# Other homes for the adaLN tiles of a two-layer hybrid decoder trunk on one NeuronCore

## The chip, the cores and the metric

The kernel runs on one NeuronCore of a Trainium2 chip. The metric is device time in microseconds of one launch; the kernel before has a median of 2782.91 us over three runs (2778.63 to 2790.88). Beside these stands one profiled execution, from which all rows below come.

Names of engines: PE is TensorE's matmul, PEld its weight load, DVE is VectorE, ACT is ScalarE, POOL is GpSimd, SP is SyncE, which issues nearly all DMAs.

## The reference

Two layers, 256 tokens of width 2048, float32. Each layer is a token mixer and then a SwiGLU feed-forward, and each of these four sub-layers has an adaLN modulation:

```python
def _ada(c, w, b):
    mod = jax.nn.silu(c) @ w + b                 # w: 2048 x 6144, one for each of the 4 sub-layers
    shift, scale, gate = jnp.split(mod, 3, axis=-1)

for layer in range(2):
    shift, scale, gate = _ada(c, ada_w[layer, 0], ada_b[layer, 0])
    h = x * (1.0 + scale) + shift
    y = _mixer_ab(h, ...) if layer % 2 == 0 else _mixer_cd(h, ...)
    x = _layer_norm(ALPHA * x + (1.0 + gate) * y, ln_g[layer, 0], ln_b[layer, 0])
    shift, scale, gate = _ada(c, ada_w[layer, 1], ada_b[layer, 1])
    y = (jax.nn.silu(h2 @ wg) * (h2 @ wu)) @ wd  # h2 = x * (1 + scale) + shift; D_FF 5632
    x = _layer_norm(ALPHA * x + (1.0 + gate) * y, ln_g[layer, 1], ln_b[layer, 1])
```

The first mixer holds mLSTM heads and RWKV-7 heads, the second retention heads and gated DeltaNet heads. `c` is one row, so an adaLN product is a vector times a matrix: 6144 dot products of length 2048 for each sub-layer, and 50 MB of weights that are read for it.

## The kernel before

**Weights.** Every large product is cut into units. A unit is one weight tile of 128 x 2048 float32 (1 MiB), brought by one DMA of SP (L681, in `raw`) into a ring of three 8 KB tiles with the tag `raw`. `split` (L703, L704) cuts it into two halves; for each half ACT writes a rounded `hi` and DVE the rest `lo`, into rings of three tiles each. PE multiplies `hi` and `lo` with the split activations in three passes (`part`, L718 to L720), 24 matmuls of 512 columns for a unit. A `raw` tile is free again when the second `lo` of its unit has been made.

**adaLN.** An adaLN unit is also a tile of 128 x 2048 (128 of the 6144 dot products). `ada_unit` loads it through the same `raw` ring, and one DVE instruction (L640, SCALAR_TENSOR_TENSOR) multiplies it with `silu(c)` and sums along the row. There are 192 units, 48 to a sub-layer. They aren't done where they are used but in small portions beside the products: after each unit of a product `fill(rate)` adds `rate` to a credit, and each whole credit emits one adaLN unit. After each norm the first 8 fills are passed over. The first feed-forward has 88 units of gate and up weights (`gu`) and 44 of down weights (`dn`), in thirds of 32 + 16, 32 + 16 and 24 + 12; in the kernel before only the `gu` products fill, at a rate of 64/84. In the second mixer (68 units) the rate is 32/44 up to a limit, in the second feed-forward 16/40 up to the last of the 192.

**Small tiles.** In the mixers, `z` is a ring of six 1 KB tiles (shifted RWKV channels), `sp` one 2 KB tile (rows on their way to DRAM), and `zt` a ring of two 4 KB tiles: rows of a product before they are transposed, or a pair of `hi` and `lo` in the first units of a stage. In the feed-forwards these tiles hold nothing after the first units.

**What sets the order.** The program is written stage by stage, and then `Plan` walks over all its instructions with a table of durations and emits an order for each engine: among the ready instructions of an engine the one with the lowest priority number goes first, a tile is opened only when its ring has a free one, and a load counts as ready only with a free tile. Splits of weights have their priorities moved forward. That order is then imposed on all engines and on SP's queue, which issues its DMAs strictly in this order, each when the tile it writes is free. So an edit of tiles or rates in one place can move instructions of every engine there.

Of the kernel before, what the change touches and what calls it, by code (L numbers as in the profile page):

```python
# [207 lines left out]
class Plan:  # L208
# [3 lines left out]
    def __init__(self, tc, nc, soon=0.5):  # L212
# [3 lines left out]
        self.depend()  # L216

# [308 lines left out]
class Trunk:  # L526
# [67 lines left out]
    def setup(self):  # L594
# [25 lines left out]
        self.ada_next = self.ada_pause = 0  # L620

# [8 lines left out]
    def ada_unit(self, u, deep):  # L630
        nc, v = self.nc, self.nc.vector
        sub, i = divmod(u, 48)
        src = self.ins["ada"][u]
        if deep and i % 2:
            w = self.a8([P, D])
            nc.sync.dma_start(w[:], src)
        else:
            w = self.raw(src)
# [40 lines left out]
    def raw(self, src, room=None):  # L679
        w = room([P, 2048]) if room else self.raw_p.tile([P, 2048], F32, tag="raw", name=self.name("raw"))  # L680
        self.nc.sync.dma_start(w[:, :src.shape[-1]], src)  # L681
        return w

    def split(self, src, n, ahead=2000, homes="ss", room=None):
# [3 lines left out]
        with self.tc.high_priority(offset=ahead):  # L688
            w = self.raw(src, room)
            parts = []  # L690
            for i, home in enumerate(homes):
# [8 lines left out]
                else:  # L700
                    hi, lo = (self.own([P, 1024], "zt", 2, F32R) for _ in range(2))
# [239 lines left out]
    def ffn(self, l, x, h):  # L941
# [3 lines left out]
        rate = 64.0 / 84 if l == 0 else 16.0 / 40  # L945
# [3 lines left out]
        for third, m in enumerate(THIRDS):  # L949
# [21 lines left out]
            for n in range(4):  # L971
                u0 = l * 44 + d0 + n * m
                banks = self.product([dn[u0 + i] for i in range(m)], 512, a, 0.0, tail=FFN_TAIL if third == 2 and n == 3 else ())
# [142 lines left out]
    def by_tokens(self, banks, zt=None):  # L1116
        if zt is None:
            zt = self.own([P, NT, 512], "zt", 2)
        for t in range(NT):
            self.nc.scalar.activation(zt[:, t, :], banks[t][:], AF.Copy)  # L1120
        return zt

    def put_by(self, banks):

        dst = self.dram.tile([T, 512], F32, name=self.name("by"))
        for t in range(NT):
            s = self.own([P, 512], "sp", 1)
            self.nc.scalar.activation(s[:], banks[t][:], AF.Copy)
            self.nc.scalar.dma_start(dst[P * t:P * t + P, :], s[:])
# [8 lines left out]
    def rwkv_tiles(self, zt, block):  # L1138

        nc = self.nc  # L1140
        for i in range(0, 4, 2):
# [5 lines left out]
            for j in range(2):  # L1147
                c, what = divmod(4 * block + i + j, 3)
                m = self.rkv[c, what] = self.own([P, T], "z", 6)
                cases.append((m[:], b[:, T * j:T * j + T], (("mu_r", "mu_k", "mu_v")[what], c)))  # L1150
# [20 lines left out]
    def rwkv_front(self, B, c):  # L1171
# [20 lines left out]
        nc.scalar.activation(sq[:], km[:], AF.Square, scale=self.col("k_k", c))  # L1192
# [5 lines left out]
        v.scalar_tensor_tensor(ar[:, ct, :, 0, :], tok(km[:]), self.nkk[:, c:c + 1], gg[:, :, 0:P], ALU.mult, ALU.mult)  # L1198
        v.tensor_tensor(ar[:, ct, :, 1, :], tok(rm[:]), gg[:, :, 1:P + 1], ALU.mult)
        kp = self.f1([P, T])  # L1200
        v.tensor_scalar(kp[:], a[:], self.col("k_a", c), self.nkk[:, 8 + c:9 + c], ALU.mult, ALU.add)
        v.tensor_tensor(kp[:], kp[:], km[:], ALU.mult)
        v.tensor_tensor(bk[:, ct, 1], tok(kp[:]), gi[:], ALU.mult)
        v.scalar_tensor_tensor(a[:], km[:], self.col("k_k", c), a[:], ALU.mult, ALU.mult)
        v.tensor_tensor(bk[:, ct, 0], tok(a[:]), gi[:], ALU.mult)
        v.scalar_tensor_tensor(kp[:], rm[:], self.col("r_k", c), kp[:], ALU.mult, ALU.mult)
        b = self.bank("c")
        nc.tensor.matmul(b[:, 0:T], self.con("bones"), kp[:], start=True, stop=True)
        v.tensor_tensor(B["vb"][:, 1, ct, :], b[:, 0:T], vm[:], ALU.mult)
# [158 lines left out]
    def rwkv(self, product, early, beside, after):  # L1368

        self.rkv = {}  # L1370
# [536 lines left out]
```

## Time and profile before

| what | value |
|---|---|
| median of 3 runs | 2782.91 us |
| the profiled execution | 2782.83 us, its span 2780.7 us |
| PE busy | 2639.4 us, 95% of the span |
| DVE busy | 2010.2 us, 72% |
| ACT busy | 1265.2 us, 45% |
| first feed-forward, first to last group of its transposes (L963) | 773.9 to 1406.2 us of the span |
| second feed-forward, the same | 2078.9 to 2698.1 us |
| second mixer, products and heads | about 1490 to 1905 us |

The span is the time from the first to the last instruction; 2.1 us of the execution lie around it. Matmuls overlap, so a busy PE can still lose time between matmuls. A row of waits names the waiting instruction, the one that released it, the total in us, how often, and the longest.

### The profile page before, as it was taken

The numbers are of one execution on the slowest core, as the hardware profiler recorded it, in microseconds if no ns is written. First come the engines' busy times: TensorE is split into PE (matmuls) and PEld (weight loads), VectorE is DVE, ScalarE is ACT, GpSimd is POOL, SyncE is SP. The second block draws the span as 40 slices with busy tenths as digits, with TensorE's granted clock in tenths as the row PEclk, the third lists the DMA queues.
The fourth block names the chain that finished last, engine by engine and source line by source line (L and its number), as shares of the span: only waits on it lengthen the run. The fifth ranks groups of instructions, "written<-read, shape, count | busy, mean of one in ns | idle before, by whom it ended". The sixth has DMA issues, their size and how long they took to land.

```text
span 2780.7 us, 33791 instructions
## 1 busy us (share of the span) xinstructions
PE 2639.4 (95%) x12906; PEld 2157.6 (78%) x12906; DVE 2010.2 (72%) x3153; ACT 1265.2 (45%) x1704; POOL 78.8 (3%) x88
## 2 busy tenths in 40 slices
PE   5598999999999999999999999999999999999997
PEld 3576777788777887788888888878778888888886
DVE  7899877658777567768767898875866646557557
ACT  2364445556634444443446554444454444443442
POOL 0000000110000000000000201100000000000000
PEclk9899999999999999999999999999999999999999
DMA  9988775235578678878866776675657657666554
GB/s 394 364 295 299 261 255 208 91 107 197 199 286 318 226 266 319 317 259 309 324 232 214 257 258 228 250 268 181 232 196 270 244 197 264 220 215 237 199 183 165
DMA packets 109820, 681.61 MB, mean 245 GB/s; under 512 B 12437, under 2 KB 15705, under 8 KB 31577
## 3 DMA queue, kind: packets, MB, share of 16 engines
q1 hardware_dynamic: 108506, 677.36, 67.0%
q8 instruction: 101, 1.65, 0.2%
q10 hardware_dynamic: 1152, 2.10, 0.2%
q14 instruction: 61, 0.50, 0.1%
HBM read 668.89 MB, written 10.52 MB: 244 GB/s over the span
## 4 chain that ended last, share of the span: by engine, by line
PE 63%; DMA 10%; DVE 9%; issue 4%; ACT 3%; POOL 0%; DVEq 0%; ACTq 0%; SPq 0%; POOLq 0%
PE g L720 19%; PE g L719 19%; PE g L718 19%; DMA raw<-ada 3%; DVE lo L704 3%; DMA raw<-gu 3%; DVE raw L640 3%; DMA raw<-w_cd 2%; ACT hi L703 2%; DMA t<-x 1%; PE m L963 1%; DMA t<-lnrow 1%; DMA raw<-w_ab 1%; PE m L1231 0%; PE m L899 0%
## 5 line engine op out<-in xcount | busy, mean ns | idle before, releaser
L704 DVE TENSOR_TENSOR lo<-raw,hi 128x1024 fp32r<-128x1024 f32 (+2 forms) x802 | 971.4, 1217 | 598.5 <-ACT hi L703 594.1
L703 ACT ACTIVATE hi<-raw 128x1024 fp32r<-128x1024 f32 (+2 forms) x802 | 838.1, 1052 | 1143.6 <-PE g L720 855.6
L718 PE MATMUL g<-hi,h 128*128 128x512 f32 (+2 forms) x2312 | 908.4, 394 | 54.8 <-ACT h L782 38.4
L719 PE MATMUL g<-lo,h 128*128 128x512 f32 (+2 forms) x2312 | 909.9, 394 | 10.2 <-DVE lo L704 9.9
L720 PE MATMUL g<-hi,h 128*128 128x512 f32 (+2 forms) x2312 | 906.2, 392 | 0.0
L718 PEld LDWEIGHTS g<-hi,h 128*128 128x128 f32 x2312 | 439.7, 190 | 152.0 <-ACT h L782 41.3
L719 PEld LDWEIGHTS g<-lo,h 128*128 128x128 f32 x2312 | 440.4, 190 | 107.8 <-DVE lo L704 20.6
L720 PEld LDWEIGHTS g<-hi,h 128*128 128x128 f32 x2312 | 440.1, 190 | 86.3 <-issue 1.7
L640 DVE SCALAR_TENSOR_TENSOR raw<-raw,silu_c 128x2048 f32<-128x2048 f32 x176 | 402.6, 2287 | 31.5 <-DMA raw<-ada 22.7
L718 PE MATMUL g<-hi,a 128*128 128x512 f32 x920 | 361.0, 392 | 5.4 <-DVE t L860 5.4
L719 PE MATMUL g<-lo,a 128*128 128x512 f32 x920 | 360.0, 391 | 0.1
L720 PE MATMUL g<-hi,a 128*128 128x512 f32 x920 | 360.0, 391 | 0.0
L718 PEld LDWEIGHTS g<-hi,a 128*128 128x128 f32 x920 | 173.4, 188 | 41.7 <-DVE t L860 5.8
L719 PEld LDWEIGHTS g<-lo,a 128*128 128x128 f32 x920 | 173.5, 189 | 36.4 <-DVE lo L704 0.9
L720 PEld LDWEIGHTS g<-hi,a 128*128 128x128 f32 x920 | 173.4, 189 | 35.7
L1413 DVE SCALAR_TENSOR_TENSOR f<-c,cols_sb,f 128x253 f32<-128x253 f32 (+2 forms) x120 | 56.0, 476 | 4.7 <-ACT f L1410 3.9
L1614 POOL TENSOR_SCALAR s<-cons_sb,log_alpha 128x128 f32<-128x128 f32 x16 | 15.2, 962 | 1017.7 <-DVE log_alpha L1558 882.9
L1084 POOL TENSOR_SCALAR_AFFINE_SELECT a<-a 128x512 f32<-128x512 f32 (+1 forms) x20 | 27.3, 1372 | 323.1 <-ACT a L1233 178.7
L640 DVE SCALAR_TENSOR_TENSOR a<-a,silu_c 128x2048 f32<-128x2048 f32 x16 | 36.3, 2285 | 0.0
L902 ACT ACTIVATE t<-m,affine 128x128 f32<-128x128 f32 x96 | 35.0, 473 | 0.1
L1231 PE MATMUL m<-y 64*128 64x256 f32 x128 | 29.2, 405 | 3.8 <-DVE a L1234 3.7
L966 ACT ACTIVATE a<-m 128x512 fp32r<-128x512 f32 x44 | 26.1, 592 | 13.5 <-PE m L963 12.3
(476 smaller groups left out, 2052.9 us busy)
## 6 DMA issues: line engine op xcount, KB each, us to landing
raw<-ada SPq DMA_DIRECT2D x176, 1024.0 KB, 5.1
raw<-gu SPq DMA_DIRECT2D x176, 1024.0 KB, 4.9
raw<-dn SPq DMA_DIRECT2D x88, 1024.0 KB, 4.8
raw<-w_cd SPq DMA_DIRECT2D x60, 1024.0 KB, 4.8
raw<-w_ab SPq DMA_DIRECT2D x48, 1024.0 KB, 5.1
a<-ada SPq DMA_DIRECT2D x16, 1024.0 KB, 17.0
raw<-o_ab SPq DMA_DIRECT2D x16, 1024.0 KB, 4.8
raw<-o_cd SPq DMA_DIRECT2D x16, 1024.0 KB, 5.4
```

The lines of the kernel that those rows point to most:

```text
L640: v.scalar_tensor_tensor(w[:], w[:], 1.0, self.sc[:], ALU.mult, ALU.mult, accum_out=m[:, i:i + 1])
L703: nc.scalar.activation(hi[:, :2 * n], ws, AF.Copy)
L704: nc.vector.tensor_tensor(lo[:, :2 * n], ws, hi[:, :2 * n], ALU.subtract)
L718: mm(o, ah, wh, start=start and k == 0, stop=False)
L719: mm(o, ah, wl, start=False, stop=False)
L720: mm(o, al, wh, start=False, stop=stop and k == 3)
L902: nc.scalar.activation(h32[:, j, :], b[:, P * j:P * j + P], AF.Identity, bias=self.ab[:, sub + 1, 16 + k:17 + k], scale=self.ab[:, sub + 1 ...
L963: nc.tensor.transpose(b[:, P * k:P * k + P], gs[:, t, P * k:P * k + P], self.ident)
L966: nc.scalar.activation(act[:, 0, :, ts], bv, AF.Copy)
L1084: self.nc.gpsimd.affine_select(x, x, pattern=[[0, n] for n in dims] + [[1, P]], compare_op=ALU.is_gt if strict else ALU.is_ge, fill=0.0, b ...
L1231: mm(b[:, T * x:T * x + T], bk[r, c, x, t, :], ar[r, c, t].rearrange("p x s -> p (x s)"), start=True, stop=True)
L1413: v.scalar_tensor_tensor(o[:, d:T], b[:, T * j:T * j + T - d], self.col(wname, 4 * (tile0 + i + j) + 3 - d), o[:, d:T], ALU.mult, ALU.add)
```

## The change

Four edits, all in where tiles live and when the adaLN units are emitted:

1. The six `z` tiles and the `sp` tile become slots of one 8 KB tile `za`, and the two `zt` tiles become halves of one 8 KB tile `zt`. The order in which slots are used stays.
2. In both feed-forwards an adaLN unit is loaded into `za` or `zt` in turn and no longer into `raw`; in the second mixer every other one goes to `za`, the rest to `raw`. The first mixer keeps `raw`.
3. Such a load is tied, for the planner alone, to the weight load that stands before it in the program: it counts as ready only when that one has landed in the plan.
4. In the first feed-forward the rate falls from 64/84 to 64/100, and the `dn` products of the first third fill too (in both feed-forwards).

```diff
-    def __init__(self, tc, nc, soon=0.5):
+    def __init__(self, tc, nc, soon=0.5, after={}):
...
+        at = {x.name: i for i, x in enumerate(self.ins)}
+        for x, y in after.items():
+            self.deps[at[x]].add(at[y])
...
+        elif home == "raw":
+            w = self.raw(src)
         else:
-            w = self.raw(src)
+            w = self.own([P, D], home, 1)
+            self.after[nc.sync.dma_start(w[:], src).ins.name] = self.load
...
     def raw(self, src, room=None):
-        self.nc.sync.dma_start(w[:, :src.shape[-1]], src)
+        self.load = self.nc.sync.dma_start(w[:, :src.shape[-1]], src).ins.name
...
-                    hi, lo = (self.own([P, 1024], "zt", 2, F32R) for _ in range(2))
+                    both = self.own([P, 2, 1024], "zt", 1, F32R)
+                    hi, lo = both[:, 0], both[:, 1]
...
     def ffn(self, l, x, h):
-        rate = 64.0 / 84 if l == 0 else 16.0 / 40
+        self.homes, self.pair = ("za", "zt"), None
+        rate = 64.0 / 100 if l == 0 else 16.0 / 40
...
-                banks = self.product([dn[u0 + i] for i in range(m)], 512, a, 0.0, tail=FFN_TAIL if third == 2 and n == 3 else ())
+                banks = self.product([dn[u0 + i] for i in range(m)], 512, a, 0.0 if third else rate, tail=FFN_TAIL if third == 2 and n == 3 else ())
...
-            zt = self.own([P, NT, 512], "zt", 2)
+            zt = self.half([P, NT, 512])
...
+    def half(self, shape):
+        if self.pair is None:
+            self.pair = self.own([P, 2, 1024], "zt", 1)
+            self.turn = 0
+        self.turn += 1
+        x = self.pair[:, self.turn % 2]
...
-            s = self.own([P, 512], "sp", 1)
+            s = self.chan[:, 6:8].rearrange("p a b -> p (a b)")
...
-                m = self.rkv[c, what] = self.own([P, T], "z", 6)
+                m = self.rkv[c, what] = self.chan[:, self.made % 6]
+                self.made += 1
...
     def rwkv(self, product, early, beside, after):
+        self.chan = self.own([P, 8, T], "za", 1)
+        self.made = 0
...
     def mixer_cd(self, h, rate):
+        self.homes, self.pair = ("za", "raw"), None
```

The order moves at three places. In the rows, `raw_N<-gu` is the load of a gate or up unit, `raw_N<-ada`, `za_N<-ada` and `zt_N<-ada` are loads of adaLN units, and `lo_N<-raw_M,hi_K` is DVE's half of a split.

**First place: the first third of the first feed-forward, shortly after its first transposes.** SP's queue before:

```order
L681 DMA raw_6269<-gu 128x2048
L681 DMA raw_6303<-ada 128x2048
L681 DMA raw_6306<-gu 128x2048
L681 DMA raw_6340<-ada 128x2048
L681 DMA raw_6343<-gu 128x2048
```

The same stretch of SP's queue now (the numbers of tiles differ, since fewer are made):

```order
L690 DMA raw_6261<-gu 128x2048
L690 DMA raw_6295<-gu 128x2048
L647 DMA zt_6329<-ada 128x2048
L690 DMA raw_6337<-gu 128x2048
L690 DMA raw_6374<-gu 128x2048
L647 DMA za_6371<-ada 128x2048
```

Before, the tile of `raw_6340` is the one that `raw_6269` leaves, three loads earlier, and two of the three are adaLN's. Now the tile of `raw_6374` is the one that `raw_6261` leaves, and the three are all weights. DVE's order there before, from the last reader of `raw_6269` on (L967 is the split of the activation):

```order
L704 TENSOR_TENSOR lo_6276<-raw_6269,hi_6275 128x1024
L967 TENSOR_TENSOR a_6216<-m_6226,a_6216 128x4x128
L704 TENSOR_TENSOR lo_6309<-raw_6306,hi_6308 128x1024
L640 SCALAR_TENSOR_TENSOR raw_6340,modulation<-raw_6340,silu_c 128x2048
L704 TENSOR_TENSOR lo_6313<-raw_6306,hi_6312 128x1024
L704 TENSOR_TENSOR lo_6346<-raw_6343,hi_6345 128x1024
```

And DVE's order now, from the last reader of `raw_6261` on:

```order
L714 TENSOR_TENSOR lo_6268<-raw_6261,hi_6267 128x1024
L649 SCALAR_TENSOR_TENSOR zt_6329,modulation<-zt_6329,silu_c 128x2048
L714 TENSOR_TENSOR lo_6298<-raw_6295,hi_6297 128x1024
L714 TENSOR_TENSOR lo_6302<-raw_6295,hi_6301 128x1024
L714 TENSOR_TENSOR lo_6340<-raw_6337,hi_6339 128x1024
L649 SCALAR_TENSOR_TENSOR za_6371,modulation<-za_6371,silu_c 128x2048
L714 TENSOR_TENSOR lo_6344<-raw_6337,hi_6343 128x1024
L714 TENSOR_TENSOR lo_6377<-raw_6374,hi_6376 128x1024
```

What moved: between the row that frees a `raw` tile and the row that reads the next load of that tile stand two rows before (`raw_6340`) and six now (`raw_6374`).

**Second place: the down products of the same third.** SP's queue there held nothing but loads of `dn` before. Now:

```order
L690 DMA raw_7232<-dn 128x2048
L690 DMA raw_7270<-dn 128x2048
L690 DMA raw_7307<-dn 128x2048
L647 DMA zt_7304<-ada 128x2048
L647 DMA za_7341<-ada 128x2048
L690 DMA raw_7344<-dn 128x2048
L690 DMA raw_7378<-dn 128x2048
L690 DMA raw_7419<-dn 128x2048
L647 DMA zt_7412<-ada 128x2048
```

Ten adaLN loads stand among the 16 of `dn`, often two in a row. Over the first feed-forward it is 61 now (15, 10, 21 and 15 in the stretches `gu`, `dn`, `gu`, `gu`) and was 60 (18, none, 24, 18).

**Third place: the second mixer.** SP's queue before, in the gated DeltaNet part:

```order
L681 DMA raw_12531<-w_cd 128x2048
L681 DMA raw_12565<-ada 128x2048
L681 DMA raw_12568<-w_cd 128x2048
L681 DMA raw_12602<-ada 128x2048
L681 DMA raw_12605<-w_cd 128x2048
L681 DMA raw_12639<-w_cd 128x2048
```

And now:

```order
L690 DMA raw_12486<-w_cd 128x2048
L690 DMA raw_12520<-ada 128x2048
L690 DMA raw_12523<-w_cd 128x2048
L690 DMA raw_12560<-w_cd 128x2048
L647 DMA za_12557<-ada 128x2048
L690 DMA raw_12594<-w_cd 128x2048
```

Of 36 adaLN loads in this stage, all in `raw`, there are now 35, 18 in `raw` and 17 in `za`. The orders of PE, DVE and ACT in this stage differ in many places, and ACT loads its function tables twice more.

32 lines of the change are left out of this document (19 added, 13 removed).

## The prediction

> **What bounds the kernel now.** The first page comes first, for the engine that is busiest:
>
> ```profile
> span 2780.7 us, 33791 instructions
> PE 2639.4 (95%) x12906; PEld 2157.6 (78%) x12906; DVE 2010.2 (72%) x3153; ACT 1265.2 (45%) x1704; POOL 78.8 (3%) x88
> PE 63%; DMA 10%; DVE 9%; issue 4%; ACT 3%; POOL 0%; DVEq 0%; ACTq 0%; SPq 0%; POOLq 0%
> PE g L720 19%; PE g L719 19%; PE g L718 19%; DMA raw<-ada 3%; DVE lo L704 3%; DMA raw<-gu 3%; DVE raw L640 3%; DMA raw<-w_cd 2%; ACT hi L703 2%; DMA t<-x 1%; PE m L963 1%; DMA t<-lnrow 1%; DMA raw<-w_ab 1%; PE m L1231 0%; PE m L899 0%
> ```
>
> The chain of waits gives 3% each to adaLN loads, `gu` loads and the adaLN passes on DVE (L640), some 9% or 250 us. That isn't what removing them would bring: while the chain follows them back, PE works on units that are already in its buffers. What PE loses has to be read from PE. The kernel holds its own yardstick: the two feed-forwards do the same products, one with 60 adaLN units beside them, the other with 16. The line of their transposes (L963) marks the same place in both, here first for the first and then for the second feed-forward (count, shortest, median and longest in ns, first and last start in us), and then both stretches in busy time (PE, PEld, DVE, ACT, POOL; clock; DMA share and GB/s):
>
> ```profile
> L963 PE MATMUL m<-cons_sb,q x88: 270/272/329, 774.2 to 1407.5; 128*128 128x128 f32 x88
> L963 PE MATMUL m<-cons_sb,q x88: 270/272/332, 2079.2 to 2699.4; 128*128 128x128 f32 x88
> 773.90:1406.20 632.30, 624.82 (x2771) 511.00 (x2770) 454.40 (x446) 261.09 (x273) 0.00 (x0) 1.00 0.80 294
> 2078.90:2698.10 619.20, 619.20 (x2770) 512.33 (x2770) 356.98 (x338) 263.94 (x273) 0.00 (x0) 1.00 0.63 226
> ```
>
> The two stretches run from first to last group of the transposes, with 2,770 matmuls each and the full clock. In the second PE is busy for all of 619.2 us. The first takes 632.3 us: **13.1 us more**, of which 7.5 us show as idle PE and the rest is hidden under the overlap of matmuls. That is all that a better supply can bring there. Why it is late is told by SP's queue and by ACT, for the first stretch and then for the second:
>
> ```profile
> SPq L681 <- DVE lo L704: 348.8, 109, 6.6
> SPq L681 <- DVE raw L640: 172.1, 55, 5.7
> L703 ACT ACTIVATE hi<-raw 128x1024 fp32r<-128x1024 f32 x225 | 235.2, 1059 | 351.0 <-PE g L720 177.7 <-DMA raw<-gu 151.1 <-DMA raw<-dn 12.2
> ...
> SPq L681 <- DVE lo L704: 510.8, 111, 6.0
> SPq L681 <- DVE raw L640: 40.6, 16, 6.8
> L703 ACT ACTIVATE hi<-raw 128x1024 fp32r<-128x1024 f32 x225 | 238.8, 1061 | 352.1 <-PE g L720 350.4 <-DVE lo L704 1.7
> ```
>
> In the second feed-forward ACT waits for PE alone: the weights are there, and PE sets the pace. In the first it waits 151.1 us for `gu` loads, and SP issues loads late since 55 times the tile that is next in the ring is held by an adaLN pass. So this stage is bound by PE with a ring of three tiles that is too short for 1.7 loads per unit, by a little.
>
> **The first feed-forward.** Durations, from the same stretch:
>
> ```profile
> L704 DVE TENSOR_TENSOR lo<-raw,hi 128x1024 fp32r<-128x1024 f32 x224 | 271.3, 1223 | 160.5 <-ACT hi L703 159.1
> L640 DVE SCALAR_TENSOR_TENSOR raw<-raw,silu_c 128x2048 f32<-128x2048 f32 x60 | 137.2, 2287 | 10.0 <-DMA raw<-ada 9.3
> L967 DVE TENSOR_TENSOR a<-m,a 128x512 fp32r<-128x512 f32 x20 | 13.4, 683 | 0.0
> DMA to landing us min/median/max: 4.7/5.2/7.9
> DMA to landing us min/median/max: 4.7/6.1/8.7
> DMA to landing us min/median/max: 4.6/4.8/5.9
> ```
>
> The landings are those of adaLN loads and of `gu` loads in the first feed-forward, and of `gu` loads in the second. A unit is 2 `lo`, so each stretch holds 112 units, and PE's pace is 619.2 / 112 = 5.53 us a unit. Now the rows of the order at the first place. Before, `raw_6340` can be issued when `lo_6276` is done, and its reader stands two rows on: 0.68 + 1.22 = 1.9 us of DVE work to cover a landing of 5.2 us. `raw_6343` follows it at once and is read four rows on (a, lo, the pass, lo: 5.4 us), less 1.06 us for ACT's `hi`, against 6.1 us. Both are short, and only what PE has in its three `hi` and `lo` tiles bridges it. After the change the weight load `raw_6374` is issued when `lo_6268` is done and read six rows on: two passes and four `lo`, 2 x 2.29 + 4 x 1.22 = 9.5 us, less 1.06 for `hi`, against 6.1 us. The adaLN load behind it, `za_6371`, has four rows, 2.29 + 3 x 1.22 = 6.0 us against 5.2. Weights have 2.3 us to spare, adaLN about 0.8 us. I therefore expect this stage to run near the pace of the second feed-forward. Not all of it:
>
> ```profile
> PE g L719 <- DVE lo L704: 3.6, 8, 0.8
> PE m L963 <- DVE q L960: 2.6, 4, 1.1
> PE g L718 <- ACT hi L703: 0.7, 2, 0.4
> ```
>
> Of 6.9 us named, 2.6 us are transposes that wait for DVE's product `q`, which may stand behind an adaLN pass of 2.29 us; that stays possible at 0.64 passes a unit. I leave 1.6 us of the 13.1 and take **-11.5 us**, with bounds of 0 (nothing cured) and -13.1.
>
> **The spread into the down products.** Ten adaLN units now stand beside 16 `dn` units of the first third, 88 us at PE's pace. DVE there: 32 x 1.22 + 10 x 2.29 = 62 us of 88. Loads: 26 MiB in 88 us is 308 GB/s, above the stage's mean of 294 but under what the start moves:
>
> ```profile
> 0.00:70.00 70.00, 35.83 (x116) 24.93 (x116) 53.56 (x62) 19.37 (x26) 0.19 (x4) 0.90 0.97 394
> ```
>
> So it lies under PE, at nothing. If that cover fails, each of the ten costs up to the 2.7 us that 1 MiB takes at 394 GB/s: 27 us at worst. In the second feed-forward the same spread moves 6 of 16 units, where PE waits for nothing and DVE is busy 357 of 619 us: 0.
>
> **The second mixer.** Here waits are of many kinds; the stretch of its products, then its PE waits, and its two spells at low clock:
>
> ```profile
> 1490.00:1905.00 415.00, 405.30 (x2276) 340.39 (x2276) 342.05 (x681) 201.85 (x313) 41.19 (x36) 0.98 0.68 245
> PE g L719 <- DVE lo L704: 2.6, 3, 1.1
> PE m L1615 <- POOL s L1614: 2.0, 2, 1.8
> PE g L718 <- ACT hi L703: 0.8, 1, 0.8
> ACT hi L703 <- DMA raw<-w_cd: 34.9, 13, 5.2
> 1563.80:1570.60 6.80, 6.80 (x35) 6.65 (x35) 6.50 (x14) 2.39 (x6) 0.00 (x0) 0.52 0.60 212
> 1686.70:1693.50 6.80, 6.80 (x27) 5.93 (x27) 6.18 (x16) 2.37 (x6) 0.00 (x0) 0.52 0.10 18
> ```
>
> PE is idle for 9.7 of 415 us, and 3.4 us of it is for weights (2.6 + 0.8). With the hidden part of the feed-forward (13.1 / 7.5) that is 6 us at most. With half of the adaLN loads still in `raw`, and the order of four engines changed, I take 2.5 us of it. Each spell at half clock loses about 3.3 us; a changed order could drop both or add as many. Bounds: 9.7 + 2 x 3.3 = 16 us gained, and as an estimate from the same rows the weight waits doubled and two more spells, 10 us lost. Two more ACT table loads of 1.28 us each hide in an ACT that is busy 202 of 415 us; without cover 2.6 us, inside these bounds. (In the Trainium skill, "TensorE: Matmul & The Clock Gate", Part 1, an idle window of about 3.4 us halves the clock until a busy one; the 0.52 in the two rows agrees with a spell of two windows. By that rule an order with fewer long stalls gains the clock as well.)
>
> ```profile
> L1415 ACT ACT_TABLE_LOAD x7 | 9.0, 1283 | 0.1
> ```
>
> **The rest.** The front, the first mixer and both output products keep their DMA order; slots of `za` and halves of `zt` are as many as the tiles they replace. Only a few transposes of the first mixer move by some rows: 0, give or take 2 us.
>
> **Sum.** -11.5 - 2.5 = -14.0 us on the profiled execution's 2782.8 us, which is also the median of the three runs (2782.91): **2769 us**.
>
> **Rivals.**
>
> *The delay moves to DVE (2779 us).* DVE is strictly in order; a pass of 2.29 us stands in front of a `lo` or a `q` whatever tile it reads, and after the change two passes sometimes stand with one `lo` between. For it: the 2.6 us at L963. Against it: ACT's 151.1 us for `gu` loads, a supply problem. If DVE were the reason, the stage would keep its excess but for the thinner rate, 0.64 against 0.76: 13.1 x 0.16 = 2 us gained, with some 2 in the mixer: 2779 us.
>
> *The mixer gains too (2758 us).* The weight waits vanish (6 us) and one or two low spells go (3.3 to 6.6 us), with 13 us in the feed-forward: some 25 us. For it: the ring is the same and the second mixer holds 36 adaLN loads. Against it: the spells lie at groups of one-column matmuls that the order keeps together.
>
> *Transfers in front of weights (2800 us, slower).* SP's queue is one line. An adaLN load with its own tile goes out as soon as the plan says, and the next weight load stands behind it, or behind two at the second place: two loads and the weight's own are 3 x 2.7 = 8 us of transfer, plus about 2 us to land, against 11 us that two loaded units give. If the real landing is later than planned, the weight is late and PE waits. From 0.23 us per adaLN load in the first feed-forward on (14 / 61) the gain is gone; at 0.5 us it is 30 us lost against 14 gained, 2800 us. For it: in the first feed-forward `gu` loads land at 6.1 us, in the second at 4.8. Against it: at 308 GB/s the queue empties faster than PE eats. (The Trainium skill, "DMA: Bandwidth & Descriptors", section "Queues, rings and completion order", says that the loads of one issuing engine share one ring on each DMA engine, consumed in ring order, so an early adaLN load does delay the weight behind it; 6.1 against 4.8 us agrees.)
>
> **Chances.** Forecast 55%, own range 2764 to 2774; DVE 22%; mixer too 15%; transfers 8%. What a measurement of this kernel tells from no change is about 0.5%, 13.9 us, so the border is at 2769, inside the forecast. Faster by over 0.5%: half of 55 and the 15, rounded to 0.43; slower by over 0.5%: 0.07; the rest, 0.50, within. The range of 8 in 10 leaves out the far half of the bigger gain and the slow case: 2757 to 2780.
>
> **What would show it.** In the first feed-forward the stretch from first to last L963 group should shrink from 632.3 to about 621 us, ACT's wait for `gu` loads from 151 us to under 30, and SP should wait for `lo` nearly alone. If ACT's wait goes and the stretch doesn't shrink, DVE was the reason, and the wait at L963 will be larger. If `gu` loads land later than 6.1 us and ACT waits for `dn` loads, it is the transfers. The second mixer should end about 2.5 us sooner after the first feed-forward than now, and the second feed-forward keep 619 us. The prediction fails above all if the second mixer's new order moves by more than 5 us, either way.

## The result, and the profile after

The changed kernel takes **2760.83 us** (median of 9 runs, 2753.68 to 2773.79). The kernel before takes 2784.07 us in 9 runs beside it (2776.68 to 2790.88). The ratio is 0.9915, with a 95% interval of 0.9894 to 0.9935: 23 us, or 0.85%, faster. The forecast was 2769, with a range of 2757 to 2780. The profiled execution of the changed kernel took 2755.91 us.

First the page of the changed kernel (busy time of each engine, then shares of the chain of waits by engine and by line):

```profile
span 2754.2 us, 33686 instructions
PE 2627.3 (95%) x12906; PEld 2155.3 (78%) x12906; DVE 2005.0 (73%) x3153; ACT 1272.4 (46%) x1706; POOL 76.8 (3%) x88
PE 75%; DVE 6%; issue 3%; DMA 3%; ACT 2%; POOL 0%; DVEq 0%; SPq 0%; ACTq 0%; POOLq 0%
PE g L730 23%; PE g L728 23%; PE g L729 23%; DVE lo L714 1%; PE m L974 1%; ACT hi L713 1%; DMA t<-x 1%; DMA t<-lnrow 1%; DMA za<-ada 1%; DVE raw L649 0%; PE m L1254 0%; PE m L909 0%; PE c L1432 0%; DVE t L870 0%; DMA raw<-w_ab 0%
```

The DMA share of the chain fell from 10% to 3%, some 195 us, while the span fell by 26.5 us. The loads were on the chain for far longer than they held PE up, as the prediction had said of its 9%.

Where the 26.5 us went is seen by cutting both spans at the same four marks: the first transposes behind each norm (L899 before, L909 after). The rows are the front with the first mixer, the first feed-forward, the second mixer with its output product, and the second feed-forward (stretch, its length, then busy time of PE, PEld, DVE, ACT, POOL; clock; DMA share and GB/s). Before:

```profile
0.00:722.30 722.30, 629.70 (x3465) 501.10 (x3465) 578.22 (x1210) 353.59 (x587) 37.63 (x52) 0.95 0.67 247
722.30:1470.80 748.50, 738.17 (x3280) 602.79 (x3280) 533.30 (x574) 322.10 (x358) 0.00 (x0) 1.00 0.76 280
1470.80:2027.20 556.40, 536.80 (x2872) 447.79 (x2872) 451.70 (x878) 271.25 (x411) 41.19 (x36) 0.98 0.66 236
2027.20:2777.10 749.90, 734.73 (x3289) 605.89 (x3289) 446.68 (x494) 318.25 (x351) 0.00 (x0) 0.99 0.61 216
```

and after:

```profile
0.00:718.10 718.10, 627.65 (x3465) 498.31 (x3465) 578.56 (x1209) 353.30 (x587) 39.58 (x52) 0.95 0.67 248
718.10:1455.00 736.90, 732.74 (x3280) 604.30 (x3280) 533.40 (x576) 325.38 (x358) 0.00 (x0) 1.00 0.77 285
1455.00:2000.80 545.80, 532.17 (x2872) 446.57 (x2872) 445.92 (x877) 275.36 (x413) 37.23 (x36) 0.98 0.65 238
2000.80:2750.60 749.80, 734.74 (x3289) 606.07 (x3289) 446.83 (x494) 318.41 (x351) 0.00 (x0) 0.99 0.60 217
```

The first feed-forward is 11.6 us shorter, the second mixer 10.6, the front 4.2, and the second feed-forward 0.1. Of the front's 4.2 us, 3.4 are clock: its spells at half clock (a spell costs half its length) lose 37.5 us before and 34.1 after. In the second mixer they lose 10.2 us in both, so its 10.6 us aren't clock. The same four stretches, less half of what their spells last inside them, are called **net** below. That is a convention: PE stands idle in part of some spells (for 4.4 of the 10.2 us from 1964.3 us on in the changed kernel), and where only the busy part is counted as half lost, the second mixer's gain is 8.8 us.

**First feed-forward.** The transposes' line and the stretch from its first to its last group, in the first feed-forward and then in the second:

```profile
L974 PE MATMUL m<-cons_sb,q x88: 270/272/331, 773.0 to 1392.0; 128*128 128x128 f32 x88
L974 PE MATMUL m<-cons_sb,q x88: 270/273/332, 2052.7 to 2673.0; 128*128 128x128 f32 x88
772.70:1390.60 617.90, 616.37 (x2758) 509.99 (x2757) 450.59 (x445) 263.31 (x272) 0.00 (x0) 1.00 0.80 300
2052.40:2671.70 619.30, 619.28 (x2771) 512.54 (x2770) 357.11 (x338) 264.15 (x273) 0.00 (x0) 1.00 0.62 225
```

It has come down to the pace of its yardstick. (It holds 13 matmuls fewer than the second; at 0.23 us each that is 3.0 us, so 620.9 us is the fair figure, against 632.3 before.) ACT's `hi` in that stretch, DVE's passes there, and what SP's queue waits for in it:

```profile
L713 ACT ACTIVATE hi<-raw 128x1024 fp32r<-128x1024 f32 x223 | 236.8, 1062 | 345.7 <-PE g L730 345.7
L649 DVE SCALAR_TENSOR_TENSOR zt<-zt,silu_c 128x2048 f32<-128x2048 f32 x30 | 68.5, 2284 | 0.7 <-DMA zt<-ada 0.7
L649 DVE SCALAR_TENSOR_TENSOR za<-za,silu_c 128x2048 f32<-128x2048 f32 x30 | 68.5, 2284 | 0.6 <-DMA za<-ada 0.6
SPq L690 <- DVE lo L714: 501.3, 107, 7.9
SPq L690 <- DVE affine L667: 17.1, 3, 6.6
```

The 151.1 us that ACT waited for `gu` loads are gone: it waits for PE alone, as it did in the second feed-forward. No load waits for an adaLN pass any more, where 55 did. From issue to landing the loads of `gu`, and then those of adaLN, take in that stretch:

```profile
DMA to landing us min/median/max: 4.6/4.7/6.4
DMA to landing us min/median/max: 6.8/7.0/10.3
```

Before it was 6.1 for `gu` and 5.2 for adaLN. The order has turned round: now the weight goes first and adaLN stands behind it. Of the 61 adaLN loads of this stage (norm to norm) 60 are now issued less than 1 us after another load of 1 MiB, before it was none of 60. It was 22 of the weight loads then, and those landed in 6.2 us at the soonest.

**Second mixer.** ACT's `hi` there (norm to norm) and PE's named waits, before and then after:

```profile
L703 ACT ACTIVATE hi<-raw 128x1024 fp32r<-128x1024 f32 x147 | 155.0, 1060 | 204.2 <-PE g L720 149.6 <-DMA raw<-w_cd 34.9 <-DVE a L1013 7.4
PE g L718 <- DVE t L860: 5.4, 1, 5.4
PE g L719 <- DVE lo L704: 2.6, 3, 1.1
PE m L1615 <- POOL s L1614: 2.0, 2, 1.8
```

```profile
L713 ACT ACTIVATE hi<-raw 128x1024 fp32r<-128x1024 f32 x147 | 155.5, 1061 | 191.5 <-PE g L730 175.3 <-DMA raw<-gu 4.8 <-DVE e L1020 3.8
PE g L728 <- DVE t L870: 5.8, 1, 5.8
PE m L909 <- ACT y L904: 2.1, 2, 1.7
PE m L1449 <- DVE q L1795: 1.6, 1, 1.6
PE g L729 <- DVE lo L714: 0.5, 1, 0.5
PE m L1640 <- POOL s L1639: 0.2, 1, 0.2
```

ACT's wait for `w_cd`, 34.9 us, is no longer among its main ones; PE's wait for `lo` fell from 2.6 to 0.5 us, that for POOL's `s` from 2.0 to 0.2. The longest one, for `t` of the norm, stays.

### The profile page after: what moved, and what is told of

It is laid out like the page before. It is cut to its first block, busy times and chain, and to the rows that moved or that the text cites. A ratio compares the mean times of both kernels' runs of the same rounds, so it can differ in the third digit from the quotient of the medians.

```text
span 2754.2 us, 33686 instructions
## 1 busy us (share of the span) xinstructions
PE 2627.3 (95%) x12906; PEld 2155.3 (78%) x12906; DVE 2005.0 (73%) x3153; ACT 1272.4 (46%) x1706; POOL 76.8 (3%) x88
## 4 chain that ended last, share of the span: by engine, by line
PE 75%; DVE 6%; issue 3%; DMA 3%; ACT 2%; POOL 0%; DVEq 0%; SPq 0%; ACTq 0%; POOLq 0%
PE g L730 23%; PE g L728 23%; PE g L729 23%; DVE lo L714 1%; PE m L974 1%; ACT hi L713 1%; DMA t<-x 1%; DMA t<-lnrow 1%; DMA za<-ada 1%; DVE raw L649 0%; PE m L1254 0%; PE m L909 0%; PE c L1432 0%; DVE t L870 0%; DMA raw<-w_ab 0%
## 5 line engine op out<-in xcount | busy, mean ns | idle before, releaser
L649 DVE SCALAR_TENSOR_TENSOR raw<-raw,silu_c 128x2048 f32<-128x2048 f32 x82 | 187.4, 2286 | 16.5 <-DMA raw<-ada 8.7
L649 DVE SCALAR_TENSOR_TENSOR za<-za,silu_c 128x2048 f32<-128x2048 f32 x56 | 127.9, 2284 | 3.5 <-DMA za<-ada 3.5
L649 DVE SCALAR_TENSOR_TENSOR zt<-zt,silu_c 128x2048 f32<-128x2048 f32 x38 | 86.8, 2284 | 1.4 <-DMA zt<-ada 1.4
L912 ACT ACTIVATE t<-m,affine 128x128 f32<-128x128 f32 x96 | 34.9, 470 | 0.1
```

Source lines behind the costliest of these rows:

```text
L649: v.scalar_tensor_tensor(w[:], w[:], 1.0, self.sc[:], ALU.mult, ALU.mult, accum_out=m[:, i:i + 1])
L912: nc.scalar.activation(h32[:, j, :], b[:, P * j:P * j + P], AF.Identity, bias=self.ab[:, sub + 1, 16 + k:17 + k], scale=self.ab[:, sub + 1 ...
```

## The experiments

The theory was that loads of adaLN in the ring of weights make the weights late, so that homes of their own cure the first feed-forward and perhaps the mixer. Its rivals: the thinner spread does it; DVE's passes do it; and, for the mixer, the planner's new order does it by luck.

All kernels in one table. Each run lists its mean granted clock, so beside the ratio of the times stands a second measure, the mean over the timed runs of **time x clock**, less that of the kernel before in the same comparison (2723.7 to 2726.7 us there; for the changed kernel, whose comparison doesn't list it, their mean, 2725.2). It tells the work apart from the clock as far as time at half clock does half the work; its standard error is 1 to 2 us for each kernel. Stages are those of the profiled execution, the first feed-forward as it was and the second mixer net.

| kernel | ratio of the times, 95% interval | time x clock, us | mean clock | first feed-forward, us | second mixer net, us |
|---|---|---|---|---|---|
| before | 1 | 0 | 0.979 | 748.5 | 546.2 |
| changed | 0.9915 [0.9894, 0.9935] | -20.1 | 0.9793 | 736.9 | 535.6 |
| tiles_only | 0.9996 [0.9976, 1.0016] | +1.2 | 0.9802 | 754.6 | 550.1 |
| spread_only | 0.9978 [0.9956, 1.0000] | -4.9 | 0.9792 | 747.6 | 545.0 |
| ffn_homes | 0.9922 [0.9895, 0.9949] | -14.7 | 0.9810 | 737.7 | 544.2 |
| ffn_half | 0.9916 [0.9884, 0.9949] | -18.0 | 0.9800 | 737.9 | 538.6 |
| no_tie | 1.0023 [0.9999, 1.0047] | -4.2 | 0.9745 | 738.9 | 539.3 |
| mix_homes | 0.9995 [0.9976, 1.0015] | -4.2 | 0.9775 | 747.9 | 541.5 |
| mixer_raw | 0.9967 [0.9943, 0.9992] | -13.3 | 0.9774 | 739.7 | 544.5 |
| mix_all_za | 0.9933 [0.9906, 0.9960] | -15.3 | 0.9791 | 737.5 | 542.1 |
| after_s0 | 0.9981 [0.9961, 1.0000] | -12.9 | 0.9755 | 745.7 | 537.8 |
| raw_s0 | 1.0029 [1.0009, 1.0049] | -6.0 | 0.9739 | 742.8 | 547.2 |
| after_s500 | 1.0001 [0.9988, 1.0014] | -1.0 | 0.9779 | 744.0 | 543.3 |
| raw_s500 | 1.0030 [1.0008, 1.0052] | +2.1 | 0.9762 | 743.6 | 545.5 |

### The tiles alone (tiles_only)

The changed kernel with all adaLN loads back in `raw` and the old rates:

```diff
-        self.homes, self.pair = ("za", "zt"), None
-        rate = 64.0 / 100 if l == 0 else 16.0 / 40
+        self.homes, self.pair = ("raw",), None
+        rate = 64.0 / 84 if l == 0 else 16.0 / 40
...
-                banks = self.product([dn[u0 + i] for i in range(m)], 512, a, 0.0 if third else rate, tail=FFN_TAIL if third == 2 and n == 3 else ())
+                banks = self.product([dn[u0 + i] for i in range(m)], 512, a, 0.0, tail=FFN_TAIL if third == 2 and n == 3 else ())
@@ def mixer_cd
-        self.homes, self.pair = ("za", "raw"), None
+        self.homes, self.pair = ("raw",), None
```

> Edit 1 alone: z and sp become slots of za, the two zt tiles become halves; all adaLN units stay in raw, with the rates of before. Theory (the shared ring of three raw tiles is what costs time, in both stages): nothing changes, -2 to +2 us on the whole; the first feed-forward keeps about 748 us from the norm before it to the norm after it, the second mixer with its output product about 556 us. Rival (the gain of the second mixer is only what a new plan happens to give): the second mixer's order differs from before, so its length moves by several us, perhaps by the whole 10.

Measured: 0.9996, and ACT waits for weights in the first feed-forward much as before. Its `hi` there (norm to norm here and in the next rows), in the kernel before and then in this one:

```profile
L703 ACT ACTIVATE hi<-raw 128x1024 fp32r<-128x1024 f32 x256 | 268.1, 1059 | 390.5 <-PE g L720 216.0 <-DMA raw<-gu 151.1 <-DMA raw<-dn 12.2
L713 ACT ACTIVATE hi<-raw 128x1024 fp32r<-128x1024 f32 x256 | 267.3, 1059 | 399.8 <-PE g L730 218.7 <-DMA raw<-gu 158.0 <-DMA raw<-dn 10.9
```

Joining the small tiles gains nothing by itself. The two stages didn't stay where they had been expected: the first feed-forward is 6.1 us longer than before and the mixer 2.3, though the time doesn't show it. So a stage of one execution can move by some us without any of the causes tested here.

### The spread alone (spread_only)

As above, but with the new rate and the portions beside `dn` kept.

```diff
@@ def ffn
-        self.homes, self.pair = ("za", "zt"), None
+        self.homes, self.pair = ("raw",), None
@@ def mixer_cd
-        self.homes, self.pair = ("za", "raw"), None
+        self.homes, self.pair = ("raw",), None
```

> Edit 1, and the new rate of 64/100 with the down products of the first third filling too; all adaLN units stay in raw. Theory of the ring: 0.64 adaLN units beside each weight unit in place of 0.76 lengthen the time that a tile has by 7 per cent, so a small part of the first feed-forward's excess goes: 744 to 748 us, the whole -1 to -4 us. Rival (the even spread is what brings it): about 738 us, the whole -10 us or more.

```profile
L713 ACT ACTIVATE hi<-raw 128x1024 fp32r<-128x1024 f32 x256 | 269.2, 1060 | 394.9 <-PE g L730 248.8 <-DMA raw<-gu 112.9 <-DMA raw<-dn 30.2
```

ACT still waits 143 us for weights, against 169 in tiles_only: the wait is thinner beside `gu` and moves to `dn`. The stage goes from 754.6 to 747.6 us against tiles_only, one profiled execution each; against the kernel before it is 0.9 us. The whole gains 4.9 us of time x clock, and the interval of the ratio 0.9978 just reaches 1. The spread doesn't cure the stage.

### The homes of the feed-forwards alone (ffn_homes)

Old rates, second mixer in `raw`; only the feed-forwards use `za` and `zt`.

```diff
-        rate = 64.0 / 100 if l == 0 else 16.0 / 40
+        rate = 64.0 / 84 if l == 0 else 16.0 / 40
...
-                banks = self.product([dn[u0 + i] for i in range(m)], 512, a, 0.0 if third else rate, tail=FFN_TAIL if third == 2 and n == 3 else ())
+                banks = self.product([dn[u0 + i] for i in range(m)], 512, a, 0.0, tail=FFN_TAIL if third == 2 and n == 3 else ())
@@ def mixer_cd
-        self.homes, self.pair = ("za", "raw"), None
+        self.homes, self.pair = ("raw",), None
```

> Edit 1, and adaLN units of the feed-forwards alone go to za and zt; rates of before (64/84, down products fill nothing), the second mixer keeps raw. Theory of the ring: the first feed-forward takes about 737 us in place of 748.5, the second mixer stays at 556, the whole -11 to -12 us. Rival (the thinner and more even spread is what brings it): the first feed-forward keeps 745 us or more. Rival (DVE's passes are in the way): it keeps 744 us or more, and the transposes' waits for DVE grow.

```profile
L713 ACT ACTIVATE hi<-raw 128x1024 fp32r<-128x1024 f32 x256 | 271.8, 1062 | 380.6 <-PE g L730 376.2 <-DVE y L862 1.7 <-DVE lo L714 1.7
```

The stage falls to 737.7 us and the wait for weights is gone, with the old rate. The passes and the loads are as many as before, and DVE is busy for 531.6 us of the stage against 533.3, so neither the work on DVE nor the number of transfers was the cause. Compared with mixer_raw below, which adds the spread to these homes, time x clock is 2712.0 in both: with the homes no worth of the spread can be seen (the standard error of that difference is some 2 us).

### Half of the homes (ffn_half)

The changed kernel, but every second adaLN unit of the feed-forwards goes through `raw`.

```diff
-        self.homes, self.pair = ("za", "zt"), None
+        self.homes, self.pair = ("za", "raw"), None
```

> The change with every other adaLN unit of the feed-forwards in za and the rest in raw, zt not used. Then raw carries 1.32 loads a unit in the first feed-forward, less than the 1.4 at which the second feed-forward of the kernel before ran without a stall. Theory of the ring: the first feed-forward takes 737 to 739 us as in the change, ACT waits for weights under 20 us. Rival (each adaLN unit that shares the ring costs its part): half of the gain is lost, 742 to 744 us, and ACT waits some 70 us for weights.

```profile
L713 ACT ACTIVATE hi<-raw 128x1024 fp32r<-128x1024 f32 x256 | 271.7, 1062 | 389.3 <-PE g L730 360.4 <-DMA raw<-gu 16.6 <-DVE lo L714 6.0
```

ACT waits 16.6 us for `gu`, and PE doesn't feel it: 737.9 us, and the whole is level with the changed kernel (0.9916). So the ring of three carries about 1.3 loads per unit here and not 1.6 to 1.7. One 8 KB tile, with half of the adaLN units still in `raw`, would have been enough for the feed-forward.

### Without the tie (no_tie)

```diff
-        plan = Plan(tc, tc.nc, 250, k.after)
+        plan = Plan(tc, tc.nc, 250)
```

> The change without the planner's tie of an adaLN load to a weight load. In SP's queue the loads into za then run far ahead, up to the output product of the first mixer, those into zt as soon as it is free. Theory (a home of its own is what counts, the tie only spaces the loads): the first feed-forward takes 737 to 740 us, but the stretch of the output product and the norm before it is longer by 2 to 8 us since adaLN loads stand in front of its rows. Rival (loads that run ahead stand in front of weights and cost PE time): the first feed-forward takes 745 us or more, the whole is no better than before.

The front of this kernel, then the adaLN passes from `za` that DVE makes in it, and SP's wait for them in the front's last third (from 500 us on):

```profile
0.00:743.60 743.60, 636.37 (x3465) 502.77 (x3465) 625.11 (x1255) 354.27 (x587) 43.97 (x52) 0.93 0.73 272
L649 DVE SCALAR_TENSOR_TENSOR za<-za,silu_c 128x2048 f32<-128x2048 f32 x23 | 52.6, 2286 | 7.9 <-DMA za<-ada 7.9
SPq L647 <- DVE za L649: 77.6, 17, 7.7
```

Without the tie the planner sends 23 adaLN loads of the first feed-forward ahead into the first mixer's last products and its output product, where the changed kernel has none. SP's single queue then stands 77.6 us in front of an adaLN load whose tile is still being read, with loads of weights behind it. The front grows from 718.1 to 743.6 us, and the first feed-forward, at 738.9, gains what it gained before. The sum is no gain: 1.0023.

What the 25.5 us of the front are made of, the traces tell in part. Spells at half clock lose 49.5 us in it, against 34.1 in the changed kernel: 15.4 us. PE is idle for 23.9 us of the last third, against 5.7. Late weights are not what shows most there: ACT waits for a weight of the output product once (6.4 us), and PE's two largest waits in that third are for DVE. Their rows come first below, and then one of the places in order of time, with start, length and, in brackets, PE's wait:

```profile
PE g L729 <- DVE lo L714: 5.5, 3, 3.8
PE m L1449 <- DVE q L1559: 5.5, 3, 2.8
689.38 2.29 DVE L649 SCALAR_TENSOR_TENSOR za<-za,silu_c 128x2048 f32<-128x2048 f32 x1
691.59 1.22 DVE L714 TENSOR_TENSOR lo<-raw,hi 128x1024 fp32r<-128x1024 f32 x1
692.86 0.80 PE L729 MATMUL g<-lo,a 128*128 128x512 f32 x1 [3.81 <-DVE lo L714]
```

An adaLN pass stands on DVE directly in front of the `lo` that PE waits for, and a pass stands just ahead of PE's two next longest waits there too (2.9 us for an `a` at 507.7 and 2.8 for a `q` at 700.5). So the loads that run ahead bring their passes with them into a stage where PE waits for DVE. The queue's share in the 25.5 us was not shown.

Of the 31.3 us between this median (2792.14) and the changed kernel's, 16 are time x clock and the rest is a clock of 0.9745 against 0.9793.

### The homes of the second mixer alone (mix_homes)

Feed-forwards in `raw` with the old rates, the mixer in `za` and `raw`.

```diff
-        self.homes, self.pair = ("za", "zt"), None
-        rate = 64.0 / 100 if l == 0 else 16.0 / 40
+        self.homes, self.pair = ("raw",), None
+        rate = 64.0 / 84 if l == 0 else 16.0 / 40
...
-                banks = self.product([dn[u0 + i] for i in range(m)], 512, a, 0.0 if third else rate, tail=FFN_TAIL if third == 2 and n == 3 else ())
+                banks = self.product([dn[u0 + i] for i in range(m)], 512, a, 0.0, tail=FFN_TAIL if third == 2 and n == 3 else ())
```

> Edit 1, and in the second mixer alone every other adaLN unit goes to za; the feed-forwards keep raw and the rates of before. Theory of the ring: the first feed-forward stays at 748 us, the second mixer with its output product falls from 556 to about 546 us, ACT's waits for its weight loads go from 35 us to near none; the whole about -10 us. Rival (luck of the new plan): the mixer falls as well, but tiles_only moves it just as far.

Measured: 0.9995, no gain in time, where 10 us had been expected, and ACT waits 18.3 us for `w_cd`, where near none had been. Its mixer takes 562.0 us (546 expected), of which spells at half clock lose 20.5 (10.2 before). The longest:

```profile
1649.30:1662.90 13.60, 13.60 (x131) 10.75 (x129) 8.04 (x15) 5.48 (x13) 0.00 (x0) 0.51 0.26 103
```

Net of the spells it takes 541.5 us, 4.7 less than before and 8.6 less than tiles_only. Time x clock says the same: 5.4 us less than tiles_only, while its mean clock is 0.9775 against 0.9802. The homes took time off the work, and the clock of the order that came with them gave it back.

### Everything but the homes of the second mixer (mixer_raw)

```diff
@@ def mixer_cd
-        self.homes, self.pair = ("za", "raw"), None
+        self.homes, self.pair = ("raw",), None
```

> The change without its edit in the second mixer: there all adaLN units stay in raw. First theory (the homes in the second mixer bring its part): the second mixer with its output product takes 552 to 558 us in the profile in place of 545.9, and the whole is some 8 to 10 us slower than the change, ratio to the kernel before about 0.995. Second theory (the mixer's length is scattered by each new plan, and the homes there bring little): the mixer may come out anywhere from 542 to 558 us, and the ratio to before stays within 0.2 per cent of the change's 0.9915. The first feed-forward keeps about 737 us under both.

```profile
L713 ACT ACTIVATE hi<-raw 128x1024 fp32r<-128x1024 f32 x147 | 154.4, 1060 | 189.0 <-PE g L730 148.6 <-DMA raw<-w_cd 28.0 <-DVE v L820 4.0
```

ACT waits 28.0 us for `w_cd` loads again, the mixer takes 551.3 us (544.5 net, 8.9 more than in the changed kernel), and its time x clock is 7 us higher. The stage lies just under the first theory's 552 to 558; the ratio, 0.9967, is outside the 0.2% of the second.

### All of the second mixer's units in `za` (mix_all_za)

```diff
@@ def mixer_cd
-        self.homes, self.pair = ("za", "raw"), None
+        self.homes, self.pair = ("za",), None
```

> The change with all adaLN units of the second mixer in za, none in raw. Theory of the ring for the mixer: as good as the change or better, 540 to 546 us for the second mixer with its output product, ACT never waits for its weight loads; but with one tile in which a unit lies some 10 us and one unit per 7.6 us, adaLN units come later than in the change. Theory of the scattered plan: anywhere from 542 to 558 us, without regard to ACT's waits for weights.

0.9933. The mixer takes 554.1 us, where 540 to 546 had been expected, and 542.1 net: better than `raw` by 2.4 us, not better than half and half. A second half in `za` brings no more.

### Homes or luck: two more orders (after_s0, raw_s0, after_s500, raw_s500)

Every kernel so far has another order in the mixer, so two pairs were made that have the planner's constant in common and differ in the mixer's homes alone. The constant is how long an engine holds back a long instruction for a more urgent one. The diff is that of raw_s0; after_s0 has its first half alone, and the two others have 500 in place of 0.5.

```diff
-        plan = Plan(tc, tc.nc, 250, k.after)
+        plan = Plan(tc, tc.nc, 0.5, k.after)
@@ def mixer_cd
-        self.homes, self.pair = ("za", "raw"), None
+        self.homes, self.pair = ("raw",), None
```

> The changed kernel, with the planner's holding time (how long an engine that could start a long instruction waits in the plan for a more urgent one that is nearly ready) at 0.5 ns in place of 250: tiles and rates as in the changed kernel, another order of rows, above all in the second mixer. Stage of second mixer and output product, from the transposes after one norm to those after the next, less the time lost to half clock: so far 544.2 to 550.1 us in five orders with all adaLN loads of the mixer in raw, 535.6 to 541.5 in four with half of them in za. If the homes make the difference, this order lies under 542 and 4 us or more under its partner with the same holding time. If it is the luck of an order, it may lie anywhere from 536 to 550, and the partner likewise. First feed-forward 736 to 740 by both.

> The partner: the same holding time of 0.5 ns, with all adaLN loads of the second mixer in raw. By the homes: mixer stage net of half clock 543 to 550 us, 4 us or more above its partner, and the whole above the partner's by as much. By the luck of an order: anywhere from 536 to 550, above or below the partner. First feed-forward 736 to 740 by both.

> The changed kernel with the planner's holding time at 500 ns in place of 250: a third order for the same tiles. By the homes: mixer stage net of half clock under 542 us, and 4 us or more under its partner. By the luck of an order: anywhere from 536 to 550. First feed-forward 736 to 740 by both.

> The partner of the last: holding time of 500 ns, all adaLN loads of the second mixer in raw. By the homes: mixer stage net of half clock 543 to 550 us, 4 us or more above its partner. By the luck of an order: anywhere from 536 to 550, above or below the partner. First feed-forward 736 to 740 by both.

The mixer's stretch and ACT's `hi` in it, first after_s0 and then raw_s0:

```profile
1469.50:2018.50 549.00, 532.23 (x2863) 445.14 (x2863) 445.97 (x876) 277.30 (x414) 37.98 (x36) 0.98 0.65 237
L713 ACT ACTIVATE hi<-raw 128x1024 fp32r<-128x1024 f32 x146 | 154.5, 1060 | 201.5 <-PE g L730 187.2 <-DMA raw<-w_cd 7.8 <-DMA raw<-gu 4.6
```

```profile
1470.40:2032.30 561.90, 537.58 (x2863) 447.27 (x2863) 446.74 (x876) 270.99 (x410) 40.15 (x36) 0.97 0.65 232
L713 ACT ACTIVATE hi<-raw 128x1024 fp32r<-128x1024 f32 x146 | 153.8, 1059 | 200.9 <-PE g L730 167.0 <-DMA raw<-w_cd 18.4 <-DMA raw<-gu 5.1
```

and after_s500 and raw_s500:

```profile
L713 ACT ACTIVATE hi<-raw 128x1024 fp32r<-128x1024 f32 x146 | 154.5, 1061 | 200.4 <-PE g L730 178.9 <-DVE e L1022 4.4 <-DMA raw<-w_cd 4.0
```

```profile
L713 ACT ACTIVATE hi<-raw 128x1024 fp32r<-128x1024 f32 x146 | 153.9, 1061 | 195.9 <-PE g L730 166.8 <-DMA raw<-w_cd 12.4 <-DVE e L1020 4.1
```

In each pair the kernel with homes waits less for `w_cd` (7.8 against 18.4 us, 4.0 against 12.4) and has the shorter mixer net of the spells: 537.8 against 547.2, and 543.3 against 545.5. The second pair misses what the homes were to give, under 542 and 4 us apart, and by itself it isn't clear of the noise. In time x clock the homes of the mixer are worth 6.9 and 3.1 us in these pairs, 7 between the changed kernel and mixer_raw, and 5.4 between mix_homes and tiles_only. Over all kernels, six with half of the mixer's units in `za` lie between 535.6 and 543.3 us (mean 539.4) and seven with all of them in `raw` between 544.2 and 550.1 (mean 546.1), without overlap. So it is the homes, some 3 to 7 us; that the rest of the scatter is the order's doing is likely and not shown.

Both theories had the first feed-forward at 736 to 740 us in these four kernels, and it took 742.8 to 745.7. In the pair with 0.5 that is clock, since spells fall into the stage and net it is 739.3 and 738.3; with 500 it is 742.3 and 740.2 net, and the second feed-forward grew too, to 757.8 and 757.2. The constant alone thus moves the changed kernel from -20.1 us of time x clock to -12.9 and -1.0: as much as the change itself. No kernel tried is measurably faster than the changed one; ffn_half is level with it.

## Why the prediction was right, and where it wasn't

**What bounds the kernel: right.** The excess over the second feed-forward was the whole prize of that stage (13.1 us), the share of the chain (9%, 250 us) was not. The stage gained 11.6.

**First feed-forward, -11.5: right in size and cause.** Stage -11.6 us; ffn_homes alone, without the spread, gives 737.7. ACT's wait for `gu` went from 151.1 us to nothing where under 30 had been said, and SP waits for `lo` nearly alone. That the size agrees to 0.1 us is luck: five kernels with these homes and this planner's constant take 736.9 to 739.7 us, and time x clock puts the homes at 13 to 15. One step in it was wrong: adaLN loads were to land in 5.2 us with 0.8 us to spare, and they land in 7.0, since all but one now follow another load of 1 MiB directly. DVE waits only 1.3 us for them, because their lead is longer than the four rows that I had counted (6.0 us): from issue to pass it is 10.4 us for `za` and 8.7 for `zt` in the median of this stage, against 5.8 before.

**Spread into `dn`, 0: right** within the noise with the homes in place (2712.0 in ffn_homes and in mixer_raw). Without them time x clock shows a gain of 4.9 us, 6 against tiles_only. The two parts don't add.

**Second mixer, -2.5: right in mechanism, too small.** The failing step is "with half of the adaLN loads still in `raw`, and the order of four engines changed, I take 2.5 us" of a possible 6. The profiles show 10.6 (8.8 by the stricter count of the spells), the four comparisons in time x clock 3 to 7. Two things were off. Half of the loads in homes was taken for half of the cure; ffn_half and mix_all_za show that half the homes do nearly all of it, since what counts is whether the ring keeps up. And the 6 us were counted from the named waits for weights alone (3.4 us), while PE's idle time in the stage fell from 19.6 to 13.6 us (stretch less busy time), the wait for POOL's `s` with it. That these other waits fell because weights came earlier was not shown apart from the order. The prediction said that it would fail above all here; it did, to the good side.

**The rest, 0 give or take 2: right.** The front net of its spells went from 684.8 to 684.0 us, the second feed-forward from 749.9 to 749.8.

**The rivals.** *The delay moves to DVE* fell: in ffn_homes the same passes at the same rate stand in DVE's order and the stage is cured; PE's named wait for `q` in the first feed-forward is 1.7 us there against 2.6 before. In no_tie's front its mechanism does show, where passes stand in front of `lo` and `q`. *Transfers in front of weights* fell for this change: `gu` loads land sooner, not later. Half of its mechanism is real: a load directly behind another of 1 MiB lands some 2 us later, and no_tie takes 2792 us where the rival had 2800. But that the transfers cost no_tie its time was not shown. The tie is what keeps that loss away, and the prediction gave the tie no term. (The Trainium skill, "DMA: Bandwidth & Descriptors", section "Queues, rings and completion order": the descriptors of one issuing engine are consumed in ring order on each DMA engine. An adaLN load lands in 6.8 us at the soonest directly behind another load and in 4.7 when it stood in `raw`, which agrees.) It isn't the tile: no_tie's 23 loads into `za` in the front, none of them directly behind another load, land in 4.9 us in the median. *The mixer gains too* (2758) is nearest to the time, 2760.83, and right in half of its reason: the weight waits went, the low spells did not (10.2 us in both profiles).

In sum -14.0 had been predicted, and time x clock says -20.1: the feed-forward's 13 to 15 (ffn_homes, mixer_raw) and the mixer's 7. Of the missing 6 us, 4 to 5 are the mixer's term by the comparison with mixer_raw, and the rest the feed-forward's. The measured 2760.83 us lie inside the wide range and below the 2764 to 2774 that had been given 55%.

## What to carry to other kernels

When side loads share a ring with the loads that feed the busiest engine, compare the stage with a like stage that has fewer of them: the difference is what homes of their own can bring, and the ring need only be relieved to the point where it keeps up, not freed altogether. A side load with its own tile must be held back by something else, or it runs ahead into a stage that has no room for the load or for the pass that reads it. And where a planner sets the order, compare edits at several settings of it, and time x clock beside time, before a few us are put down to an edit.

## What the runs showed of the hardware that was not expected

**The clock differs from order to order, by as much as the edits bring.** The mean granted clock of a kernel's timed runs went from 0.9739 (raw_s0) to 0.9810 (ffn_homes), with 12906 matmuls in every one: time less time x clock is 73 and 53 us. The kernel before has 0.979 in each of its three comparisons. It turned a gain of 4 to 5 us (mix_homes) into none, and made 11 us between the medians of ffn_homes (2763.11) and mixer_raw (2774.56), whose time x clock is equal. Within one kernel it moves too: the changed kernel's slowest run, 2773.79 us, has a clock of 0.975, its profiled one of 2755.91 us 0.982. But for the one that each execution ends in, the spells of the profiled executions last 3.41, 6.83, 10.24, 13.65 or 17.07 us, steps of 3.41. (The Trainium skill, "TensorE: Matmul & The Clock Gate", Part 1, has a window of about 3.4 us; the steps agree.) What in an order brings a spell on was not settled.

**A us of idle PE that went was worth almost two here, and that is no rule.** In the first feed-forward PE's idle time fell by 6.2 us (10.33 to 4.16) and the stage by 11.6; in the second mixer by 6.0 for 10.6. That is a factor of 1.8 to 1.9, near the 13.1 / 7.5 from which the prediction took its 6 us; the prediction puts the rest down to the overlap of matmuls, which no run shows by itself. Between orders the factor doesn't hold: the first feed-forward has 9.7 us of idle PE both in mix_homes and in after_s500, and takes 747.9 us in one and 744.0 in the other, of which 1.7 are clock.

**A load that SP issues directly behind another takes it longer to issue**, 425 ns in the median against 327. That isn't the tile: in the changed kernel the adaLN loads that follow another issue within 0.1 us take about 425, while the 78 loads into `za` and `zt` in no_tie, which don't, take 327 or 328 in the median. It cost nothing that shows.
